# A two-layer hybrid diffusion backbone on one core: the first norm's modulation made wholly on TensorE, and the later modulation rows placed behind the input norms

## The chip, the cores and the metric

The kernel runs on one core of a Trainium2 chip as one launch. The metric is the device time of the launch in microseconds (us). Engines are named as in the profile: PE (TensorE), DVE (VectorE), ACT (ScalarE), POOL (GpSimd), and SP (SyncE), whose queue issues nearly all DMA transfers.

## What is computed

Two trunk layers run over 1024 latent tokens and 256 context tokens of width 1024, all in float32. Each layer begins with an RMS norm whose result is scaled and shifted by vectors that come from a conditioning vector (`c` for the latent tokens, `c_ctx` for the context tokens) through the matrix `w_mod`; then a combined input projection feeds four head groups (a short gated convolution, multi-head latent attention, a Conformer convolution, 2-D neighbourhood attention), an output projection merges them, and a squared-ReLU MLP follows.

```python
mod = [m[:, None, :] for m in jnp.split(jax.nn.silu(c) @ w_mod[i] + b_mod[i], N_MOD, axis=-1)]
mod_c = jnp.split(jax.nn.silu(c_ctx) @ w_mod[i] + b_mod[i], N_MOD, axis=-1)
x, xc = trunk_layer(x, xc, mod, mod_c, p, ang_row, ang_col, last=(i == DEPTH - 1))

# in trunk_layer
sh1, sc1, ga1, sh2, sc2, ga2 = mod
h = rmsnorm(x, p["g_pre_mix"]) * (1 + sc1) + sh1      # first norm
hc = rmsnorm(xc, p["g_pre_mix"]) * (1 + sc1c) + sh1c
u = h @ w_in
...
kv = heads(rmsnorm(ckv, g_kv) @ w_ukv)                 # latent keys: norm, then expansion
...
x = x + ga1 * rmsnorm(y, p["g_post_mix"])
hm = rmsnorm(x, p["g_pre_mlp"]) * (1 + sc2) + sh2
x = x + ga2 * rmsnorm(sq_relu_mlp(hm, p["w_mlp1"], p["w_mlp2"]), p["g_post_mlp"])
```

The product with `w_mod` gives 6 x 1024 numbers for each of two vectors and each layer: 48 tiles of 128. Tiles 0 to 15 are the shift and scale of the first norm; tiles 16 to 47 are wanted behind the attention. The change concerns layer 0.

## The kernel before

The tokens are kept transposed (channels on the 128 partitions, tokens along the free axis) in three segments of 512, 512 and 256 tokens (0, 1 and 2; the third is the context). Weights are split into a high and a low part, so that each product is three matmuls: `weights` loads 128x512 pieces into the ring of tiles `raw` (4 buffers), ScalarE writes the high part `wh`, GpSimd or VectorE the low part `wl`.

The modulation is made in two ways. `mod_pe` does tiles 0 to 6 on PE: for each tile a load of 512 KB into a tile `s` and eight matmuls of 128x2 (L246), and at the end one VectorE addition for each vector (L251). `mod_rows` does the others as row sums on VectorE (L288): for each tile two halves of 128x512 are loaded (L284), and for each half and each vector one scalar_tensor_tensor multiplies the half with a row of silu(c) that stands on all partitions (tiles `ya`) and adds up the row; tiles 7 to 15 use buffers of tag `s`, tiles 16 to 47 use tag `xl` (3 buffers). The rows in `ya` are made from a 4 KB load, four matmuls against ones (L264) and four Silu on ScalarE (L265).

A norm (`modulate`) squares x on ScalarE (L133), adds the squares up on VectorE (L148), sums over partitions on PE (L161), takes the root and reciprocal (L164, L165), broadcasts it on PE (L170), and then does for each of eight k-tiles two VectorE steps (L192, L194) with a ScalarE step between (L193); the trunk's matmuls read what these leave.

`layer` merges the stages: `merge` runs a main generator and lets others go on in proportion to its progress, by the numbers in RATES (`ma`, `mf`, `mv`, `mp`, `hm` belong to the modulation rows `moda`). The stage `first` holds the gate projections of segment 0 (L375 to L377) and the projection NQ of segment 0 (`na_project`, evacuated with L93 and L94 to `ge` and `pt`); behind it come the other segments, `values`, the latent projections with their norms (`mla_project`), and the heads. The instructions are emitted in this order, and a scheduler then sorts them by its own estimate of times before they are put into each engine's queue; each engine runs its queue in order. SP's queue too is in order: a load whose buffer isn't free holds up the loads behind it.

Of the kernel before, what the change touches and what calls it, by code (L numbers as in the profile page):

```python
# [6 lines left out]
AF = mybir.ActivationFunctionType  # L7
ALU = mybir.AluOpType
# [19 lines left out]
QTAG = 'xl'  # L28
PA, PD = 0, 1
WALT = (3, 2)  # L30
MPE, RM, MX = 7, 1.0, 4
ROT0, ROT1, ROT2 = 'SGSGS', 'SGSGS', 'SGSGS'
RATES = dict(pend=(1.0, 1.0), cv=(1.0, 0.862), cp=(1.0, 0.6), hr=(1.0, 0.484), hc=(0.3, 0.3), hm=(0.313, 0.679), ma=(0.195, 0.26), mf=(0.5, 0.5), mv=(0.5, 1.04), cb=(1.0, 1.3), mp=(0.5, 0.5), ar=(0.392, 0.517), ac=(0.6, 0.8), ob=(0.65, 0.696), oc=(0.575, 0.65), od=(0.65, 0.26), on=(0.6, 0.522), mb=(1.0, 0.646), pr=(0.2, 0.2), pt=(0.805, 1.12), pn=(0.612, 1.5), pm=(1.5, 1.5), mn=(1.74, 2.0), mc=(0.4, 0.325), mt=(1.0, 0.6), en=(1.0, 1.0))
PADC = 15
CFW = PADC + LAT + PADC + CTX + PADC
T5 = 1328
# [25 lines left out]
class Kern:  # L62
# [137 lines left out]
    def norm(self, y, si, o, n, l, which, acc, xsrc, xdst, nxt=None, ptag="R", tag="e2", tmp=None):  # L200
# [31 lines left out]
        if nxt:  # L232
            l2, w2, H = nxt
            yield n / 200
            yield from self.modulate(yk, n, l2, w2, v, H, o, acc, ptag, tag, tmp)


    def mod_pe(self, load):

        nc = self.nc  # L240
        ps = self.ps("O", [P, MPE, 2])
        for m in range(MPE):
            raw = self.t([P, KT, P], "s")
            nc.sync.dma_start(raw, self.a["wmod0"][m])
            for k in range(KT):
                nc.tensor.matmul(ps[:, m, :], raw[:, k, :], self.sc[:, k, :], start=k == 0, stop=k == KT - 1)  # L246
            if m == MX:
                load()
            yield 1.0
        for v in range(2):  # L250
            nc.vector.tensor_tensor(self.mods[0][v][:, 0:MPE], ps[:, :, v], self.vec[:, 0, 0:MPE], op=ALU.add)  # L251

    def mod_vectors(self, tags, pe=False):

        nc = self.nc
        out = []
        for v in range(2):
            t = self.t([P, 2, 512], tags[v])
            if pe:
                row = self.t([1, 1024], "s")  # L260
                nc.sync.dma_start(row, self.a["crow"][v:v + 1, :])
                for h in range(2):
                    ps = self.ps("S")
                    nc.tensor.matmul(ps, self.ones[0:1, :], row[:, h * 512:(h + 1) * 512], start=True, stop=True)  # L264
                    nc.scalar.activation(t[:, h], ps, AF.Silu)  # L265
                out.append([t[:, 0], t[:, 1]])
                continue
            nc.sync.dma_start(t, self.a["crow"][v:v + 1, :].rearrange("v (h c) -> v h c", h=2)
                              .to_broadcast([P, 2, 512]))
            nc.scalar.activation(t, t, AF.Silu)  # L270
            out.append([t[:, 0], t[:, 1]])
        return out

    def mod_rows(self, l, f0, f1, vecs, wtag="xl", jtag="ma"):

        nc = self.nc
        mod, part = self.mods[l], self.part
        nv = len(vecs)
        junk = self.t([P, 512], jtag) if nv > 1 else None
        a = f0  # L280
        for f in range(f0, f1):
            for h in range(2):
                w = self.t([P, 512], wtag)
                nc.sync.dma_start(w, self.a["wmodt"][l, f, :, h * 512:(h + 1) * 512])  # L284
                for v in range(nv):
                    dst = (mod if h == 0 else part)[v][:, f:f + 1]
                    q = w if v == nv - 1 else junk
                    nc.vector.scalar_tensor_tensor(q, w, 1.0, vecs[v][h], op0=ALU.mult, op1=ALU.mult,  # L288
                                                   accum_out=dst)
                yield nv * 0.6  # L290
            if f % 8 == 7 or f + 1 == f1:
                r = slice(a, f + 1)
                for v in range(nv):
                    nc.vector.tensor_tensor(mod[v][:, r], mod[v][:, r], part[v][:, r], op=ALU.add)
                    nc.vector.tensor_tensor(mod[v][:, r], mod[v][:, r], self.vec[:, l, r], op=ALU.add)
                a = f + 1
# [676 lines left out]
    def layer(self, l, H, pend):  # L973

        last = l == 1
        R = {k: v[l] for k, v in RATES.items()}
        qsegs = (0, 1) if last else (0, 1, 2)
# [4 lines left out]
        ch = self.chain  # L982
        self.cf_open(0)
        self.cf_open(1)
        moda = self.mod_rows(0, 16, 48, self.vecs) if l == 0 else iter(())
        first = ch(*[self.cf_gemm(l, H, (0,), j, j == 0 and l == 0) for j in range(2)], self.na_project(l, H, "NQ", M_NAQ, (0,)))
        if l:
            first = ch(first, self.na_project(l, H, "NK", M_NAK, (0,)))
        self.merge(first, (pend, R['pend']), (moda, R['ma']))
        self.go(pend)  # L990
        self.merge(self.cf_gemm(l, H, bsegs, 0), (moda, R['mf']))
        conv = ch(*[self.cf_conv(l, qsegs, j) for j in range(2)])
        self.merge(self.cf_gemm(l, H, bsegs, 1), (conv, R['cb']), (moda, R['mf']))
        self.merge(self.values(l, H), (conv, R['cv']), (moda, R['mv']))
        self.mla_open()
        self.merge(self.mla_project(l, H, (0, 1, 2), qsegs), (conv, R['cp']), (moda, R['mp']))
        heads = self.mla_heads(l, qsegs)
        rest1 = ch(self.na_project(l, H, "NK", M_NAK, (1, 2) if l else (0, 1, 2)), self.na_project(l, H, "NQ", M_NAQ, bsegs))
        self.merge(heads, (rest1, R['hr']), (conv, R['hc']), (moda, R['hm']))
        self.go(moda)  # L1000
        self.rot = "G"
        self.yfalloc(0)
# [103 lines left out]
    @staticmethod  # L1106
    def stats(g):

        next(g)
        next(g)  # L1110
# [7 lines left out]
    def run(self):  # L1118
# [39 lines left out]
        def load(si, tag):  # L1158
            o, n = SEGS[si]
            X[si] = Seg(pools[tag], n, F32, tag, f"x{si}")  # L1160
            for i, t in enumerate(X[si].tiles):
                kk = X[si].kk
                nc.sync.dma_start(t, a["xin"][:, i * kk:(i + 1) * kk, o:o + n])

        self.vecs = self.mod_vectors(("ya", "ya"), True)
        md = self.mod_rows(0, MPE, 16, self.vecs, wtag="s")
        H, first = {}, []

        def early():
            load(0, "ah")  # L1170
            g = self.modulate(X[0].k, 512, 0, "1", 0, lambda: H[0], 0, tmp="T")
            self.stats(g)
            first.append(g)
            self.w0 = [self.weights(a["win"][0, m], D) for m in (M_CFG, M_CFA)]

        self.merge(self.mod_pe(early), (md, RM))
        self.go(md)
        load(1, "c5")
        load(2, "ah")
        H.update({si: self.newh(SEGS[si][1]) for si in range(3)})  # L1180
        self.go(first[0])
        pend = self.chain(*[self.modulate(X[si].k, SEGS[si][1], 0, "1", int(si == 2), H[si], 0, ptag="O", tmp="T") for si in (1, 2)])
        H, pend = self.layer(0, H, pend)
        self.layer(1, H, pend)
# [103 lines left out]
```

## Time and profile before

| what | value |
|---|---|
| runs | 3201.49, 3206.51, 3210.8 us; median 3206.51 |
| the profiled execution | 3201.57 us, span 3199.6 us |
| PE busy | 2959.4 us (92%) |
| DVE busy | 2019.0 us (63%) |
| ACT busy | 1399.5 us (44%) |
| POOL busy | 1076.6 us (34%) |
| mean granted TensorE clock | 0.961 of full speed |

The span is from the first to the last instruction of the profiled execution. The busy shares are averages over stages of different make.

### The profile page before, as it was taken

The numbers are of one execution on the slowest core, as the hardware profiler recorded it, in microseconds if no ns is written. First come the engines' busy times: TensorE is split into PE (matmuls) and PEld (weight loads), VectorE is DVE, ScalarE is ACT, GpSimd is POOL, SyncE is SP. The second block draws the span as 40 slices with busy tenths as digits, with TensorE's granted clock in tenths as the row PEclk, the third lists the DMA queues.
The fourth block names the chain that finished last, engine by engine and source line by source line (L and its number), as shares of the span: only waits on it lengthen the run. The fifth ranks groups of instructions, "written<-read, shape, count | busy, mean of one in ns | idle before, by whom it ended". The sixth has DMA issues, their size and how long they took to land.

```text
span 3199.6 us, 46244 instructions
## 1 busy us (share of the span) xinstructions
PE 2959.4 (92%) x15916; PEld 2534.7 (79%) x15916; DVE 2019.0 (63%) x4128; ACT 1399.5 (44%) x2882; POOL 1076.6 (34%) x861
## 2 busy tenths in 40 slices
PE   7879889979999989889999998998989999989997
PEld 5767668878888878768888887777878888978886
DVE  8999556685753377975543689556776633654335
ACT  3313445666553364212322443555765433543332
POOL 2302122225444432223333421222334444334443
PEclk9889889989999989999999999998989999999998
DMA  7435423453533354563212443425445333534233
GB/s 264 152 120 189 118 62 101 126 148 107 159 109 96 102 186 150 193 213 107 91 60 66 145 140 126 141 76 144 151 116 146 111 96 96 172 100 147 96 97 104
DMA packets 284461, 410.01 MB, mean 128 GB/s; under 512 B 28098, under 2 KB 129474, under 8 KB 284228
## 3 DMA queue, kind: packets, MB, share of 16 engines
q1 hardware_dynamic: 284228, 407.07, 40.9%
q8 instruction: 126, 2.06, 0.3%
q14 instruction: 107, 0.88, 0.1%
HBM read 354.66 MB, written 52.30 MB: 127 GB/s over the span
## 4 chain that ended last, share of the span: by engine, by line
PE 70%; DVE 9%; DMA 5%; ACT 2%; issue 2%; SPq 1%; POOL 0%; DVEq 0%; ACTq 0%; POOLq 0%
PE G L122 11%; PE G L123 11%; PE G L124 11%; PE S L122 9%; PE S L124 9%; PE S L123 9%; PE T L675 3%; DMA xl<-in_wmodt_dram 2%; PE O L688 1%; PE O L687 1%; DVE xl L288 1%; DMA ah<-KR 1%; PE S L809 1%; PE S L758 1%; PE S L759 1%
## 5 line engine op out<-in xcount | busy, mean ns | idle before, releaser
L94 POOL TENSOR_TENSOR wl<-raw,wh 128x512 fp32r<-128x512 f32 x672 | 898.4, 1340 | 1525.7 <-ACT wh L93 1399.1
L93 ACT ACTIVATE wh<-raw 128x512 fp32r<-128x512 f32 x768 | 483.0, 631 | 847.7 <-PE S L123 391.9
L122 PE MATMUL G<-h,wh 128*128 128x512 f32 (+1 forms) x1128 | 427.0, 379 | 6.5 <-ACT h L193 2.3
L123 PE MATMUL G<-h,wh 128*128 128x512 f32 (+1 forms) x1128 | 423.0, 375 | 4.4 <-DVE h L194 4.3
L124 PE MATMUL G<-h,wl 128*128 128x512 f32 (+1 forms) x1128 | 423.4, 375 | 0.2 <-POOL wl L94 0.2
L122 PE MATMUL S<-h,wh 128*128 128x512 f32 (+1 forms) x904 | 324.6, 359 | 2.9 <-ACT h L193 1.6
L124 PE MATMUL S<-h,wl 128*128 128x512 f32 (+1 forms) x904 | 324.7, 360 | 1.4 <-POOL wl L94 1.4
L123 PE MATMUL S<-h,wh 128*128 128x512 f32 (+1 forms) x904 | 323.7, 358 | 0.0
L659 POOL TENSOR_SCALAR ah<-ah,sm 128x1280 f32<-128x1280 f32 (+3 forms) x144 | 148.2, 1033 | 410.4 <-DVE sm L658 155.2
L929 DVE TENSOR_TENSOR ac<-ac,S 128x512 f32<-128x512 f32 (+1 forms) x340 | 208.9, 617 | 114.6 <-PE S L124 113.7
L122 PEld LDWEIGHTS G<-h,wh 128*128 128x128 f32 x1128 | 215.7, 191 | 46.0 <-ACT h L193 4.7
L123 PEld LDWEIGHTS G<-h,wh 128*128 128x128 f32 x1128 | 215.2, 191 | 42.2 <-DVE h L194 6.0
L124 PEld LDWEIGHTS G<-h,wl 128*128 128x128 f32 x1128 | 215.4, 191 | 36.4 <-issue 0.7
L94 DVE TENSOR_TENSOR pt<-T,pt 128x512 fp32r<-128x512 f32 (+1 forms) x280 | 169.3, 615 | 87.9 <-ACT pt L93 86.6
L929 DVE TENSOR_TENSOR ac<-ac,G 128x512 f32<-128x512 f32 (+1 forms) x268 | 169.0, 631 | 82.1 <-PE G L124 80.9
L93 ACT ACTIVATE pt<-T 128x512 fp32r<-128x512 f32 (+1 forms) x280 | 146.5, 543 | 117.5 <-PE T L675 103.4
L122 PEld LDWEIGHTS S<-h,wh 128*128 128x128 f32 x904 | 173.9, 192 | 29.5 <-ACT h L193 2.3
L124 PEld LDWEIGHTS S<-h,wl 128*128 128x128 f32 x904 | 173.6, 192 | 27.3 <-POOL wl L94 2.7
L123 PEld LDWEIGHTS S<-h,wh 128*128 128x128 f32 x904 | 173.9, 192 | 25.6
L122 PE MATMUL G<-s,wh 128*128 128x512 f32 (+1 forms) x534 | 185.3, 348 | 2.2 <-ACT ge L863 1.7
L124 PE MATMUL G<-s,wl 128*128 128x512 f32 (+1 forms) x534 | 182.0, 341 | 3.3 <-DVE wl L94 3.2
L123 PE MATMUL G<-s,wh 128*128 128x512 f32 (+1 forms) x534 | 182.0, 341 | 0.3 <-DVE s L94 0.3
(339 smaller groups left out, 6938.9 us busy)
## 6 DMA issues: line engine op xcount, KB each, us to landing
raw<-in_w_dram SPq DMA_DIRECT2D x520, 256.0 KB, 2.6
xl<-in_wmodt_dram SPq DMA_DIRECT2D x160, 256.0 KB, 3.0
raw<-in_wout_dram SPq DMA_DIRECT2D x144, 256.0 KB, 3.0
raw<-in_win_dram SPq DMA_DIRECT2D x96, 256.0 KB, 3.1
ah<-KN SPq DMA_DIRECT2D x32, 320.0 KB, 4.9
ah<-MV SPq DMA_DIRECT2D x16, 640.0 KB, 6.4
ah<-NV SPq DMA_DIRECT2D x16, 640.0 KB, 4.9
XM<-yo SPq DMA_DIRECT2D x36, 256.0 KB, 2.9
```

Source lines behind the costliest of these rows:

```text
L93: nc.scalar.activation(hi, src, AF.Copy)
L94: (eng or nc.vector).tensor_tensor(lo, src, f32(hi), op=ALU.subtract)
L122: nc.tensor.matmul(out, wh, xh, start=i == 0, stop=False)
L123: nc.tensor.matmul(out, wh, xl, start=False, stop=False)
L124: nc.tensor.matmul(out, wl, xh, start=False, stop=i == last)
L288: nc.vector.scalar_tensor_tensor(q, w, 1.0, vecs[v][h], op0=ALU.mult, op1=ALU.mult, accum_out=dst)
L659: nc.gpsimd.tensor_scalar(p[:, :L], p[:, :L], sm[:, 9:10], 1.0, op0=ALU.mult, op1=ALU.mult)
L675: nc.tensor.transpose(T[:, i, q * P:(q + 1) * P], ps_list[q][:, cols[q]:cols[q] + P], self.ident)
L687: nc.tensor.matmul(O[:, a:b], V[:, kt, :], th[:, i, a:b], start=first, stop=False)
L688: nc.tensor.matmul(O[:, a:b], V[:, kt, :], tl[:, i, a:b], start=False, stop=last)
L758: nc.tensor.matmul(S, Qt[:, 0, q:q + P], K[0][:, ks], start=True, stop=False)
L929: nc.vector.tensor_tensor(a, a, ps, op=ALU.add)
```

## The change

`mod_pe` does all 16 tiles of the first norm (MPE = 16), 72 matmuls more; the 36 row sums of tiles 7 to 15 go. x0 is loaded at step 2 of `mod_pe` and its statistics are begun at step 12. The rows of silu(c) are made from a broadcast load of 512 KB each and one Silu of 128x1024 each, emitted behind the first norm. The modulation rows of tiles 16 to 47 take their buffers from the ring `raw`, aren't merged into the stage `first` or its pending norms any more, run at rates of their own (MODA; in RATES their entries were ma 0.195, mf 0.5, mf 0.5, mv 0.5, mp 0.5 and hm 0.313 for layer 0), and are kept in the order of the program on VectorE (`pin`).

```diff
-MPE, RM, MX = 7, 1.0, 4
+MPE, MX, MS = 16, 2, 12
+MODA = (1.0, 0.5, 0.5, 0.5, 0.3)
...
+    def pin(self, ins):
+
+        return self.tc.keep_in_program_order(ins)
+
-    def mod_pe(self, load):
+    def mod_pe(self, steps):
...
-            if m == MX:
-                load()
-            yield 1.0
+            if m in steps:
+                steps[m]()
...
-    def mod_vectors(self, tags, pe=False):
+    def mod_vectors(self, tags):
...
-            if pe:
-                row = self.t([1, 1024], "s")
-                nc.sync.dma_start(row, self.a["crow"][v:v + 1, :])
-                for h in range(2):
-                    ps = self.ps("S")
-                    nc.tensor.matmul(ps, self.ones[0:1, :], row[:, h * 512:(h + 1) * 512], start=True, stop=True)
-                    nc.scalar.activation(t[:, h], ps, AF.Silu)
-                out.append([t[:, 0], t[:, 1]])
-                continue
             nc.sync.dma_start(t, self.a["crow"][v:v + 1, :].rearrange("v (h c) -> v h c", h=2)
                               .to_broadcast([P, 2, 512]))
             nc.scalar.activation(t, t, AF.Silu)
...
-                    nc.vector.scalar_tensor_tensor(q, w, 1.0, vecs[v][h], op0=ALU.mult, op1=ALU.mult,
-                                                   accum_out=dst)
+                    self.pin(nc.vector.scalar_tensor_tensor(q, w, 1.0, vecs[v][h], op0=ALU.mult, op1=ALU.mult,
+                                                            accum_out=dst))
...
-        moda = self.mod_rows(0, 16, 48, self.vecs) if l == 0 else iter(())
+        moda = self.mod_rows(0, 16, 48, self.vecs, "raw") if l == 0 else iter(())
...
-        self.merge(first, (pend, R['pend']), (moda, R['ma']))
+        self.merge(first, (pend, R['pend']))
         self.go(pend)
-        self.merge(self.cf_gemm(l, H, bsegs, 0), (moda, R['mf']))
+        self.merge(self.cf_gemm(l, H, bsegs, 0), (moda, MODA[0]))
...
-        self.merge(heads, (rest1, R['hr']), (conv, R['hc']), (moda, R['hm']))
+        self.merge(heads, (rest1, R['hr']), (conv, R['hc']), (moda, MODA[4]))
...
-        self.vecs = self.mod_vectors(("ya", "ya"), True)
-        md = self.mod_rows(0, MPE, 16, self.vecs, wtag="s")
         H, first = {}, []
 
-        def early():
-            load(0, "ah")
+        def stats():
             g = self.modulate(X[0].k, 512, 0, "1", 0, lambda: H[0], 0, tmp="T")
             self.stats(g)
...
-        self.merge(self.mod_pe(early), (md, RM))
-        self.go(md)
+        self.mod_pe({MX: lambda: load(0, "ah"), MS: stats})
...
         self.go(first[0])
+        self.vecs = self.mod_vectors(("ya", "ya"))
```

Three places of the queues, as the scheduler leaves them. The lines of the changed kernel are its own numbers (L149 is L148 of before, L193 is L192, L283 is L288, L103 is L102).

**VectorE at the start, changed kernel.** `e_495` is the sum of x1's squares, `mod_127` and `mod_128` the vectors of the latent and the context tokens, `g` their gains, `T` the first norm's first step:

```order
L149 TENSOR_TENSOR e_495<-e_495,e_506 128x512
L149 TENSOR_TENSOR e_495<-e_495,e_509 128x512
L149 TENSOR_TENSOR e_495<-e_495,e_512 128x512
L149 TENSOR_TENSOR e_495<-e_495,e_515 128x512
L255 TENSOR_TENSOR mod_127<-O_133,vec 128x16
L255 TENSOR_TENSOR mod_128<-O_133,vec 128x16
L308 SCALAR_TENSOR_TENSOR g_395<-mod_127,vec 128x8
L308 SCALAR_TENSOR_TENSOR g_755<-mod_128,vec 128x8
L193 SCALAR_TENSOR_TENSOR T_397<-x_0_164,g_395,e_303 128x512
L193 SCALAR_TENSOR_TENSOR T_401<-x_0_164,g_395,e_303 128x512
```

In the kernel before, the additions of the vectors stood ahead of most of these sums, with row sums between them; now the two additions (L255) and the first norm stand behind x1's whole sum.

**ScalarE at the same place, changed kernel.** `e_` are x1's squares, `ya_429` and `ya_432` the rows of silu(c), `h_0` the first norm's result:

```order
L134 ACTIVATE e_509<-x_2_365 128x512
L134 ACTIVATE e_512<-x_3_366 128x512
L265 ACT_TABLE_LOAD
L265 ACTIVATE ya_429<-ya_429 128x1024
L134 ACTIVATE e_515<-x_3_366 128x512
L265 ACTIVATE ya_432<-ya_432 128x1024
L174 ACTIVATE e_303<-G_295 128x512
L194 ACTIVATE h_0_375<-T_397,mod_127 128x512
```

The last square of x1 stands between the two Silu.

**VectorE at the third segment's input norm, before.** `h_0_402` and `T_781` belong to this norm, `ma` and `xl` to modulation rows:

```order
L194 SCALAR_TENSOR_TENSOR h_3_399<-T_696,mod_127,h_3_395 128x512
L165 RECIPROCAL sm_773<-sm_773 128x2
L288 SCALAR_TENSOR_TENSOR xl_1164,mod_128<-xl_1164,ya_142 128x512
L288 SCALAR_TENSOR_TENSOR ma_532,part_131<-xl_1221,ya_133 128x512
L167 TENSOR_TENSOR e_776<-ident,sm_773 128x256
L288 SCALAR_TENSOR_TENSOR xl_1221,part_132<-xl_1221,ya_142 128x512
L288 SCALAR_TENSOR_TENSOR ma_532,mod_127<-xl_1225,ya_133 128x512
L288 SCALAR_TENSOR_TENSOR xl_1225,mod_128<-xl_1225,ya_142 128x512
L192 SCALAR_TENSOR_TENSOR T_781<-x_0_380,g_779,O_770 128x256
L192 SCALAR_TENSOR_TENSOR T_785<-x_0_380,g_779,O_770 128x256
```

**and in the changed kernel**, where `c_439` is an evacuation of the gates, `pt_667` and `pt_741` are the two evacuations of NQ, and the norm is that of `h_0_393`:

```order
L360 TENSOR_TENSOR c_439<-S_587,c_439 128x4x16x8
L195 SCALAR_TENSOR_TENSOR h_3_390<-T_676,mod_127,h_3_386 128x512
L95 TENSOR_TENSOR pt_667<-G_641,ge_666 128x512
L95 TENSOR_TENSOR pt_741<-S_715,ge_740 128x512
L166 RECIPROCAL sm_749<-sm_749 128x2
L168 TENSOR_TENSOR e_752<-ident,sm_749 128x256
L193 SCALAR_TENSOR_TENSOR T_757<-x_0_371,g_755,O_746 128x256
L193 SCALAR_TENSOR_TENSOR T_761<-x_0_371,g_755,O_746 128x256
L195 SCALAR_TENSOR_TENSOR h_0_393<-T_757,mod_128,h_0_391 128x256
L195 SCALAR_TENSOR_TENSOR h_0_393<-T_761,mod_128,h_0_391 128x256
L193 SCALAR_TENSOR_TENSOR T_765<-x_0_371,g_755,O_746 128x256
```

The row sums between the steps are gone, and the norm follows the second evacuation of NQ directly. The rows begin 16 instructions further on, behind the norm's last step.

**SP's queue at the key/value expansion's weights, before:**

```order
L284 DMA xl_1721<-in_wmodt_dram 128x512
L102 DMA raw_1995<-in_win_dram 128x512
L284 DMA xl_1725<-in_wmodt_dram 128x512
L102 DMA raw_2128<-in_wukv_dram 128x512
L284 DMA xl_1729<-in_wmodt_dram 128x512
L102 DMA raw_2144<-in_win_dram 128x512
```

**and in the changed kernel**, where `in_wmodt` are the modulation rows' loads:

```order
L279 DMA raw_2040<-in_wmodt_dram 128x512
L279 DMA raw_2044<-in_wmodt_dram 128x512
L279 DMA raw_2083<-in_wmodt_dram 128x512
L279 DMA raw_2087<-in_wmodt_dram 128x512
L279 DMA raw_2121<-in_wmodt_dram 128x512
L279 DMA raw_2125<-in_wmodt_dram 128x512
L103 DMA raw_2129<-in_wukv_dram 128x512
L103 DMA raw_2145<-in_win_dram 128x512
```

Of four buffers in the ring `raw`, the tile `raw_2129` takes the one that `raw_2083` leaves.

## Rows read from the trace of the kernel before

**Rows 1.** The busy time of each engine in four stretches and over all of them (view by stretches): the stretch, its length, the busy time and instruction count of each engine, the granted TensorE clock, the share of the DMA engines, GB/s.

```profile
0.00:54.40 54.40, 36.14 (x135) 29.52 (x136) 41.10 (x112) 17.67 (x29) 7.37 (x10) 1.00 0.90 325
54.40:134.20 79.80, 65.60 (x255) 48.52 (x256) 79.77 (x181) 33.68 (x58) 26.86 (x16) 0.89 0.47 150
134.20:240.00 105.80, 88.19 (x496) 77.99 (x495) 105.80 (x252) 21.07 (x51) 12.10 (x8) 0.90 0.39 125
240.00:357.20 117.20, 98.88 (x486) 82.00 (x485) 94.40 (x191) 36.73 (x78) 21.23 (x16) 0.90 0.54 178
0.00:357.20 357.20, 288.81 (x1368) 238.03 (x1369) 321.07 (x732) 109.14 (x216) 67.56 (x50) 0.91 0.53 178
```

**Rows 2.** The same view for the modulation rows alone (line 288 on VectorE; the accumulator read that belongs to each has its own record): the stretch, its length, VectorE busy with them and their records.

```profile
0.00:54.40 54.40, 30.13 (x81) 1.00 0.90 325
54.40:134.20 79.80, 43.63 (x103) 0.89 0.47 150
134.20:240.00 105.80, 42.25 (x116) 0.90 0.39 125
240.00:357.20 117.20, 12.19 (x30) 0.90 0.54 178
```

**Rows 3.** The timeline, around 22 to 30 us: start, duration, engine, line, operation, tiles, count. One row of GpSimd's casts and two modulation rows of VectorE.

```profile
22.41 6.49 POOL L94 TENSOR_TENSOR wl<-raw,wh 128x512 fp32r<-128x512 f32 x4 [21.47 <-ACT wh L93]
...
24.34 1.75 DVE L288 SCALAR_TENSOR_TENSOR ma<-s,ya 128x512 f32<-128x512 f32 x1
...
29.48 0.69 DVE L288 SCALAR_TENSOR_TENSOR s<-s,ya 128x512 f32<-128x512 f32 x1
```

**Rows 4.** The timeline: the matmuls of the first norm's vectors, the sums and broadcast of its statistics, and the first norm's start.

```profile
15.17 13.81 PE L246 MATMUL O<-sc,s 128*128 128x2 f32 x64
...
37.38 2.05 PE L170 MATMUL G<-e,ones 128*128 128x512 f32 x2
...
53.41 1.83 PE L161 MATMUL O<-ones,e 128*128 128x1 f32 x8 [13.98 <-DVE e L148]
...
54.49 1.41 DVE L192 SCALAR_TENSOR_TENSOR T<-x,g,e 128x512 f32<-128x512 f32 x2
...
55.44 1.26 ACT L193 ACTIVATE h<-T,mod 128x512 fp32r<-128x512 f32 x2
...
56.17 0.80 PE L375 MATMUL S<-h,wh 128*128 128x512 f32 x1 [0.93 <-ACT h L193]
...
56.58 1.17 ACT L93 ACTIVATE ah<-ah 128x1152 fp32r<-128x1152 f32 x1
```

**Rows 5.** The DMA view of 0 to 60 us: GB/s in 40 equal slices of 1.5 us, and two of the loads (KB of one, median us to landing).

```profile
GB/s 0 121 125 330 303 382 408 352 415 404 400 389 384 403 411 423 410 391 392 373 388 385 378 393 386 388 362 352 381 411 415 397 158 12 0 141 128 81 171 4
...
x<-in_xin_dram SPq DMA_DIRECT2D x10, 512.0 KB, 8.9
...
s<-in_wmod_dram SPq DMA_DIRECT2D x7, 512.0 KB, 6.8
```

**Rows 6.** The timeline: squares on ScalarE and their additions on VectorE, x0.

```profile
16.84 1.15 ACT L133 ACTIVATE e<-x 128x512 f32<-128x512 f32 x2 [0.96 <-DMA x<-in_xin_dram]
...
18.02 3.12 DVE L148 TENSOR_TENSOR e<-e,e 128x512 f32<-128x512 f32 x4 [0.54 <-ACT e L133]
```

**Rows 7.** The timeline of TensorE: successive matmuls of the trunk at three places (the spacing is the difference of the starts).

```profile
59.34 0.63 PE L377 MATMUL G<-h,wl 128*128 128x512 f32 x1
59.76 0.63 PE L375 MATMUL S<-h,wh 128*128 128x512 f32 x1
...
89.28 0.39 PE L122 MATMUL G<-h,wh 128*128 128x512 f32 x1
89.51 0.39 PE L123 MATMUL G<-h,wh 128*128 128x512 f32 x1
...
146.44 0.28 PE L122 MATMUL S<-h,wh 128*128 128x256 f32 x1
146.56 0.28 PE L123 MATMUL S<-h,wh 128*128 128x256 f32 x1
```

**Rows 8.** The timeline of VectorE: steps of the third segment's input norm (256 columns), one early and the last.

```profile
118.20 0.87 DVE L192 SCALAR_TENSOR_TENSOR T<-x,g,O 128x256 f32<-128x256 f32 x2
...
133.34 0.86 DVE L194 SCALAR_TENSOR_TENSOR h<-T,mod,h 128x256 fp32r<-128x256 f32 x2
```

**Rows 9.** The timeline: the load of the key/value expansion's weights, the third latent-norm step, and the first softmax of attention with the matmul before it.

```profile
150.00 0.33 SPq L102 DMA_DIRECT2D raw<-in_wukv_dram  x1
...
239.52 0.41 DVE L167 TENSOR_TENSOR e<-ident,sm 128x256 f32<-128x256 f32 x1
...
356.27 0.40 PE L758 MATMUL S<-ah,xl 96*128 96x512 f32 x1
...
357.18 0.69 DVE L645 TENSOR_REDUCE sm<-S 128x1 f32<-128x512 f32 x1 [0.46 <-PE S L760]
```

**Rows 10.** What VectorE waited for in 240 to 357 us: line waited by, what it waited for, us in total, times, longest.

```profile
DVE pt L94 <- ACT ge L93: 13.4, 5, 6.8
DVE ma L288 <- DMA xl<-in_wmodt_dram: 5.3, 4, 2.4
```

**Rows 11.** The view by stretches for the convolution's steps alone (line 402 on VectorE).

```profile
134.20:240.00 105.80, 54.55 (x89) 0.90 0.39 125
```

More of the change, by code (lines that the diff above doesn't have):

```diff
@@ L30 @@
 WALT = (3, 2)
-MPE, RM, MX = 7, 1.0, 4
+MPE, MX, MS = 16, 2, 12
+MODA = (1.0, 0.5, 0.5, 0.5, 0.3)
 ROT0, ROT1, ROT2 = 'SGSGS', 'SGSGS', 'SGSGS'
-RATES = dict(pend=(1.0, 1.0), cv=(1.0, 0.862), cp=(1.0, 0.6), hr=(1.0, 0.484), hc=(0.3, 0.3), hm=(0.313, 0.679), ma=(0.195, 0.26), mf=(0.5, 0.5), mv=(0.5, 1.04), cb=(1.0, 1.3), mp=(0.5, 0.5), ar=(0.392, 0.517), ac=(0.6, 0.8), ob=(0.65, 0.696), oc=(0.575, 0.65), od=(0.65, 0.26), on=(0.6, 0.522), mb=(1.0, 0.646), pr=(0.2, 0.2), pt=(0.805, 1.12), pn=(0.612, 1.5), pm=(1.5, 1.5), mn=(1.74, 2.0), mc=(0.4, 0.325), mt=(1.0, 0.6), en=(1.0, 1.0))
+RATES = dict(pend=(1.0, 1.0), cv=(1.0, 0.862), cp=(1.0, 0.6), hr=(1.0, 0.484), hc=(0.3, 0.3), cb=(1.0, 1.3), ar=(0.392, 0.517), ac=(0.6, 0.8), ob=(0.65, 0.696), oc=(0.575, 0.65), od=(0.65, 0.26), on=(0.6, 0.522), mb=(1.0, 0.646), pr=(0.2, 0.2), pt=(0.805, 1.12), pn=(0.612, 1.5), pm=(1.5, 1.5), mn=(1.74, 2.0), mc=(0.4, 0.325), mt=(1.0, 0.6), en=(1.0, 1.0))
 PADC = 15
@@ L988, in layer @@
             first = ch(first, self.na_project(l, H, "NK", M_NAK, (0,)))
-        self.merge(first, (pend, R['pend']), (moda, R['ma']))
+        self.merge(first, (pend, R['pend']))
         self.go(pend)
-        self.merge(self.cf_gemm(l, H, bsegs, 0), (moda, R['mf']))
+        self.merge(self.cf_gemm(l, H, bsegs, 0), (moda, MODA[0]))
         conv = ch(*[self.cf_conv(l, qsegs, j) for j in range(2)])
-        self.merge(self.cf_gemm(l, H, bsegs, 1), (conv, R['cb']), (moda, R['mf']))
-        self.merge(self.values(l, H), (conv, R['cv']), (moda, R['mv']))
+        self.merge(self.cf_gemm(l, H, bsegs, 1), (conv, R['cb']), (moda, MODA[1]))
+        self.merge(self.values(l, H), (conv, R['cv']), (moda, MODA[2]))
         self.mla_open()
-        self.merge(self.mla_project(l, H, (0, 1, 2), qsegs), (conv, R['cp']), (moda, R['mp']))
+        self.merge(self.mla_project(l, H, (0, 1, 2), qsegs), (conv, R['cp']), (moda, MODA[3]))
         heads = self.mla_heads(l, qsegs)
         rest1 = ch(self.na_project(l, H, "NK", M_NAK, (1, 2) if l else (0, 1, 2)), self.na_project(l, H, "NQ", M_NAQ, bsegs))
-        self.merge(heads, (rest1, R['hr']), (conv, R['hc']), (moda, R['hm']))
+        self.merge(heads, (rest1, R['hr']), (conv, R['hc']), (moda, MODA[4]))
         self.go(moda)
```

## The prediction

> **What bounds the kernel now.** The page comes first: TensorE is busy 2959.4 of 3199.6 us, so over the whole program it is the bound. But the change touches only layer 0 up to its first attention, and an average over the program says nothing of that stretch. So the second view is the table by stretches, cut at the first norm's start (54.4), the end of the third input norm (134.2), the third latent-norm step (240) and the first softmax (357.2) [rows 1]. There VectorE is the bound: 41.10 of 54.40, then 79.77 of 79.80 and 105.80 of 105.80, then 94.40 of 117.20. Between 54.4 and 240 us it has no idle time at all; before that it has 13.3 us, after it 22.8. TensorE has 50 us of gaps between 54.4 and 357.2 (302.8 less 65.6, 88.2 and 98.9). The same table for the modulation rows alone [rows 2] shows what fills VectorE: 128.20 us in 330 records, two for each of 164 instructions (one cut by a boundary counts in both stretches), 0.78 us each on average; 0.73 in the third stretch (42.25 for 58), 0.85 in the second (43.63 for 51.5). So up to the first softmax the time is VectorE's work plus VectorE's waits, and I sum the change that way; behind the softmax nothing is changed, and I let the difference pass through as it stands.
>
> **The change, part by part.**
>
> *36 row sums leave VectorE.* Tiles 7 to 15 had 9 x 2 x 2 of them. At 0.73 that is 26.3 us, at 0.85 it is 30.6. I take 0.73. The longer ones are the ones that met a GpSimd instruction: 1.75 us beside GpSimd's cast of the weights, 0.69 just behind it [rows 3]. GpSimd casts the same weights after the change, so what is taken away is the plain part. The Trainium skill ("SBUF — State Buffer", section "SBUF: two separate sides") says that a VectorE instruction with two SBUF inputs and a GpSimd instruction that reads SBUF exclude each other for a whole instruction, whichever began second waiting; the 1.75 agrees. By that rule the stretching goes over to the next such VectorE instruction and is not saved, which speaks against counting the 0.85.
>
> *72 matmuls of 128x2 come to TensorE.* One costs 13.81/64 = 0.216 us [rows 4], so all 16 tiles cost 27.6 us. In the new order TensorE does 4 tiles, waits for the sum of x0's squares, does 8 column sums (1.83), 9 tiles, two broadcasts (2.05) and 3 tiles. x0's sum: 3 tiles of wmod and 4 of x are 3.7 MB; the DMA moved 1.3 MB by 7.5 us and then about 0.59 MB per 1.5 us [rows 5], so x0 is there at some 14 us and summed at 16. From there 1.8 + 15.6 + 2.1 + 5.2 gives 41 us. This is hidden if the vectors are not wanted before 41; without that cover each tile would cost 1.7 us.
>
> *When the first norm can start.* In VectorE's new order the 7 additions of x1's squares stand ahead of the two additions that finish the vectors. Bytes ahead of x1's last tile: 16 wmod (8.4 MB), x0 (2.1), four weights (1.05), x1 (2.1), 13.6 MB in all: 7.5 + 12.3/0.394 = 39 us. A second thing is later. On ScalarE the last of x1's eight squares stands behind the Silu of the broadcast c row, and that row lies behind two context tiles and itself in the queue, 15.2 MB: 43 us. Then a Silu of 1024 columns (a 1152-wide ScalarE copy takes 1.17 [rows 4]), a square and an addition (0.58 and 0.78 at the pace of [rows 6]): some 46. The vectors and gains follow, so the first norm begins at 47 us, and the first trunk matmul, 1.7 us behind it as before (54.49 to 56.17 [rows 4]), at 49 to 50 against 56.17. Six to seven us are won on TensorE. VectorE has 14 additions and little else by then, 11 us of work, so it has idled 36.
>
> *The input norms without rows between them.* Before, two row sums stood between most norm steps, and VectorE was never out of work. Now none stands ahead of the last norm step of segment 2, and the third segment's norm stands behind the evacuation of the second NQ block in VectorE's order. That evacuation needs 144 of the trunk's 512-wide matmuls, and the third norm's broadcast another 24 behind them: 169 x 0.23 = 38.9 us at the pace of [rows 7], so 49.5 + 38.9 = 88, and 1 to 2 more for TensorE's waits for the first eight norm steps. Then 16 steps at 0.43 (two in 0.87 [rows 8]) with their handovers, 7 to 9 us: the norms end at about 99, against 134.2 before. VectorE's work in 47 to 99 is 32 wide steps of 0.7 (two in 1.41 [rows 4]), 16 narrow ones and about 12 small ones, 36 us; with the 11 before it has 47, and has idled 52 of 99. At this point it had idled 13.3 before. So 38.7 us more idle.
>
> *The rows behind it.* The 128 rows of tiles 16 to 47 all still come before the first softmax, as before: their work moves and is neither more nor less. They now take their buffers from the ring of four that the weights use. This is a new wait. The weights of the key/value expansion were loaded at 150.0 us, long before use [rows 9]; in the new order of SyncE's queue they stand behind tile 2083 in the ring, whose rows are about 40 instructions behind the third latent-norm step on VectorE. No row of before shows this wait. From below: VectorE sees nothing of it, since it is behind and TensorE catches up, 0. From above: 42 rows of 0.65 (27 us), DMA and casts of 5, less some 15 of matmuls that TensorE has between the two places: 17 per such place, and TensorE's stall counts only as far as VectorE then waits for it. I take 5. SyncE is in order, so what stands behind the waiting load (the writes of KN, further weights) waits with it; it is in the same price.
>
> *Sum.* Idle +38.7, work -26.3, ring +5: +17.4 us. The idle time of 240 to 357, 22.8 us, most of it for casts behind TensorE (13.4 [rows 10]), I leave as it is. A second way: norms end at 99; then up to the third latent-norm step VectorE has 82 rows of 0.73, 160 convolution steps of 0.613 (54.55/89 [rows 11]) and some 10 us more, so it is there at 267 (before: 239.5 [rows 9], with 149 rows and 93 convolution steps done). From there the old VectorE had 94.4 us of work [rows 1]; the new one has 46 rows left where the old had 15 (+23) and 26 convolution steps where the old had 93 (-41), so 76. TensorE has 271 matmuls of 512 columns and 188 of 256 from there to the first attention: at 0.23 and 0.12 [rows 7] 85 us. So TensorE is the longer there, and with 15 to 25 of waits (the old kernel took 117 for 79 us of such matmuls, but there VectorE had 94 us to do beside them) the softmax comes at 367 to 377, +10 to +20. I stay with the sum.
>
> The profiled execution took 3201.57 us (span 3199.6), 4.9 below the median of the runs, 3206.5. I add to the median: 3206.5 + 17.4 = 3224.
>
> **The rivals.** A measurement of this kernel tells about 0.3% (9.6 us) from no change.
>
> *Faster.* The earlier first matmul carries through, and the third norm is not held by NQ: if the norms end at 80, VectorE has idled 33 and the sum is 33 - 13.3 - 26.3 = -7; with the clock 10 less, 3190 to 3200. It decides at an end of the norms of 86.6, where the new idle equals 13.3 + 26.3. For it: the first 20 trunk matmuls ran at 0.43 us each, which is 1.2 GHz, against 0.23 later [rows 7], with a granted share of 0.89 in that stretch [rows 1]; with TensorE busy up to its start this could be 3 us less. Against it: VectorE's order is fixed. The Trainium skill ("TensorE: Matmul & The Clock Gate", section "Why this matters for your kernels") advises no idle gaps between bursts of matmuls; by that rule the added matmuls help, but TensorE waits here too between 41 and 49.
>
> *No change.* The stall at the seam is half what I think (norms end at 90), and no load waits in the ring: 43 - 39.6 = +3, 3210. For it: TensorE's gaps (50 us) can take up what comes late.
>
> *Slower still.* The shared ring stops TensorE and VectorE in turn, at the weights of the latent keys, the two query blocks and the expansion, 17 us each, partly overlapping: +30, 3237. For it: several weights in SyncE's order stand behind pinned rows. Against it: where VectorE is far behind, the wait is its own work.
>
> **How the numbers follow.** Forecast 0.42, slower still 0.18, no change 0.27, faster 0.13. The forecast's own range is 3214 to 3232. The range reaches to the faster case's near edge and beyond the slower still: 3197 to 3243. Faster by over 0.3%: most of the faster case, 0.12. Slower: the forecast, the slower still and a part of no change would be 0.6; same 0.28.
>
> **What the profile after would show.** First trunk matmul at 49 to 50 us; the two vector additions behind x1's last square; VectorE idle some 17 us between 47 and 99, waiting for TensorE's NQ block; no row before the third norm's last step; the third latent-norm step at about 267; weight loads whose issue waits for VectorE; the first softmax at 367 to 377. I would be wrong if VectorE has other work to fill the seam, if the norms end before 87, or if the idle time of 240 to 357 shrinks by as much as the early idle grows.

## The result, and the profile after

The changed kernel takes 3241.74 us (median of four runs, 3238.63 to 3244.5) against 3204.7 for the kernel before beside it: a ratio of 1.0113, with an interval of 1.0094 to 1.0132, 37 us slower. Its profiled execution took 3238.63 us, span 3236.8. The number lies inside the predicted range and the sign is the forecast one, but the step is twice the forecast 17.4, and the ledger below shows that it came about in another way: 54 us are lost by the first softmax, 29 come back in the MLP, and some 14 go again in layer 1.

The view by stretches answers to [rows 1]; the cuts are the first norm's start, the end of the third input norm, the third latent-norm step and the first softmax.

```profile
0.00:65.36 65.36, 58.23 (x267) 57.17 (x267) 11.16 (x25) 19.11 (x28) 5.66 (x10) 1.00 0.75 283
65.36:117.38 52.02, 50.26 (x204) 40.36 (x205) 39.07 (x71) 32.42 (x55) 19.13 (x12) 0.96 0.25 83
117.38:282.98 165.60, 98.62 (x524) 84.76 (x524) 156.43 (x366) 23.03 (x54) 12.94 (x10) 0.75 0.31 100
282.98:411.56 128.58, 104.34 (x513) 86.48 (x512) 81.01 (x194) 38.09 (x79) 23.67 (x18) 0.89 0.61 197
```

VectorE's work up to the softmax is 287.7 us, 33.4 less than the 321.1 of before. Its idle time is 54.2, 13.0, 9.2 and 47.6 us, 124 in all, against 36. So 87.8 more idle less 33.4 work is the 54.4 us by which the softmax is later. TensorE was starved in the third stretch, 98.6 busy of 165.6 at a granted clock of 0.75; in the first two it idles 7.1 and 1.8 us, and in the last 24.2. The modulation rows alone, in the last two stretches of after, to be read beside [rows 2] (in the first two they have 0.07 us):

```profile
117.38:282.98 165.60, 56.34 (x164) 0.75 0.31 100
282.98:411.56 128.58, 33.14 (x92) 0.89 0.61 197
```

The timeline of the start answers to [rows 4]:

```profile
6.69 13.78 PE L251 MATMUL O<-sc,s 128*128 128x2 f32 x64 [6.69 <-DMA s<-in_wmod_dram]
...
22.04 30.86 PE L251 MATMUL O<-sc,s 128*128 128x2 f32 x144
...
47.87 0.69 DVE L149 TENSOR_TENSOR e<-e,e 128x512 f32<-128x512 f32 x1 [2.19 <-ACT e L134]
...
54.60 10.24 PE L251 MATMUL O<-sc,s 128*128 128x2 f32 x48
...
64.88 0.26 DVE L255 TENSOR_TENSOR mod<-O,vec 128x16 f32<-128x16 f32 x2 [16.32 <-PE O L251]
65.36 1.42 DVE L193 SCALAR_TENSOR_TENSOR T<-x,g,e 128x512 f32<-128x512 f32 x2
...
66.98 0.77 PE L370 MATMUL S<-h,wh 128*128 128x512 f32 x1
```

x1's last addition is at 47.87, close to the 46 of the forecast. But the two additions of the vectors wait 16.3 us more for TensorE: it has 64 + 144 + 48 = 256 records, of 0.215 us each, for the program's 128 matmuls. The third group of rows answers to [rows 9]:

```profile
282.98 0.41 DVE L168 TENSOR_TENSOR e<-ident,sm 128x256 f32<-128x256 f32 x1
...
307.93 0.33 SPq L103 DMA_DIRECT2D raw<-in_wukv_dram  x1
...
411.56 0.69 DVE L640 TENSOR_REDUCE sm<-S 128x1 f32<-128x512 f32 x1 [0.43 <-PE S L755]
```

The expansion's weights are loaded at 307.9 instead of 150.0. The waits of 117 to 283 us (line waiting, what it waited for, us in total, times, longest) show the ring that the prediction spoke of: TensorE waits for the high part of a weight, and SP's queue for VectorE to leave a tile. TensorE's first, then SP's two longest:

```profile
PE S L123 <- ACT wh L94: 48.8, 3, 29.9
```

```profile
SPq L279 <- DVE raw L283: 88.4, 26, 13.4
SPq L103 <- DVE raw L283: 21.7, 9, 3.7
```

And VectorE's main wait in 283 to 411.5 us, to be read beside [rows 10]:

```profile
DVE pt L95 <- ACT ge L94: 38.2, 13, 7.3
```

Behind the softmax, the two kernels are followed by landmarks that both traces have on VectorE. The changed kernel is later by 54.4 us at the softmax, 51.3 at the last broadcast of the output norms of layer 0, 22.6 at layer 1's first norm, 24.4 at layer 1's first softmax, and 37.1 at its last instruction. So between the second and third of these, in the MLP, it gains 29 us. The stretch as a whole, of before and of after:

```profile
1187.60:1570.50 382.90, 353.86 (x1985) 307.05 (x1986) 270.75 (x591) 119.43 (x243) 109.83 (x81) 0.96 0.46 149
```

```profile
1238.90:1593.10 354.20, 345.48 (x1985) 302.07 (x1986) 266.72 (x593) 119.87 (x243) 115.24 (x81) 0.98 0.50 161
```

The same number of matmuls, in 29 us less: TensorE idles 9 us there instead of 29, and its busy time is 8 us shorter at a granted clock of 0.98 instead of 0.96.

### The profile page after: what moved, and what is told of

Same layout as the page of the kernel before. It is cut to its first block, busy times and chain, and to the rows that moved or that the text cites. A ratio compares the mean times of both kernels' runs of the same rounds, so it can differ in the third digit from the quotient of the medians.

```text
span 3236.8 us, 46444 instructions
## 1 busy us (share of the span) xinstructions
PE 2981.7 (92%) x16052; PEld 2566.8 (79%) x16052; DVE 1974.8 (61%) x4048; ACT 1403.2 (43%) x2882; POOL 1074.2 (33%) x861
## 4 chain that ended last, share of the span: by engine, by line
PE 70%; DVE 8%; DMA 4%; ACT 2%; issue 2%; SPq 1%; POOL 0%; ACTq 0%; DVEq 0%; POOLq 0%
PE G L123 11%; PE G L124 11%; PE G L125 11%; PE S L123 9%; PE S L125 9%; PE S L124 9%; PE T L670 3%; DMA ah<-KR 2%; PE O L683 1%; PE O L682 1%; PE S L804 1%; PE S L754 1%; PE S L755 1%; PE S L753 1%; DVE xl L283 1%
## 5 line engine op out<-in xcount | busy, mean ns | idle before, releaser
L123 PE MATMUL S<-h,wh 128*128 128x512 f32 (+1 forms) x904 | 327.1, 362 | 50.9 <-ACT wh L94 48.8
```

What stands on the lines that cost most here:

```text
L123: nc.tensor.matmul(out, wh, xh, start=i == 0, stop=False)
```

## The experiments

Times stand beside runs of the kernel before on the same chip (3199 to 3200 us there); at the ratio of 1.0113 the changed kernel would take 3235 to 3236 on these. "Softmax" is the first one of layer 0.

**e1, layer 1's rows unpinned.** The pin sits in a helper that layer 1's modulation rows use as well, in the MLP of layer 0.

```diff
-                    self.pin(nc.vector.scalar_tensor_tensor(q, w, 1.0, vecs[v][h], op0=ALU.mult, op1=ALU.mult,
-                                                            accum_out=dst))
+                    ins = nc.vector.scalar_tensor_tensor(q, w, 1.0, vecs[v][h], op0=ALU.mult, op1=ALU.mult,
+                                                         accum_out=dst)
+                    if l == 0:
+                        self.pin(ins)
```

> The changed kernel, with the pin kept for layer 0's modulation rows and dropped for layer 1's, which the same helper issues. In the trace after, the first softmax is 54 us later than before but the MLP of layer 0's first segment (1299 to 1593) takes 294 us against 323, and the end is 37 us later. Theory P (the pin on layer 1's rows, which spreads them over the MLP, gives these 29 us back): the MLP stretch takes 323 us again and the time is 3242 + 25 to 32, about 3270. Rival (the stretch is shorter for another reason, such as where the loads fall after a later start): the time stays within 6 us of 3242.

Measured: 3256.85 us, ratio 1.0177 (1.0158 to 1.0196), some 21 us above the changed kernel. The MLP stretch is back at 380.7 us, 26.5 longer than in the changed kernel:

```profile
1240.10:1620.80 380.70, 354.87 (x1985) 308.53 (x1986) 270.59 (x591) 119.52 (x243) 111.59 (x81) 0.96 0.45 149
```

Theory P holds for the stretch. The time rose by less than the 25 to 32 us expected, since layer 1 takes 8 us less here (1632 against 1640 from its first norm to the end).

**e2, the kernel before with layer 1's rows pinned.** The same lines, in the kernel before, with `if l == 1`.

> The kernel before, with the pin on layer 1's modulation rows alone and nothing else changed. Theory P: the MLP stretch falls from 323 to about 294 us; up to 8 of it is lost again in layer 1's attention as it was in the changed kernel, so 3205 - 20 to 29, about 3180. Rival (another reason for the shorter stretch): 3205, no change beyond 0.3%.

Measured: 3187.25 us, ratio 0.9959 (0.9945 to 0.9972). The MLP stretch takes 355.5 against 382.9:

```profile
1186.50:1542.00 355.50, 345.96 (x1985) 302.12 (x1986) 265.29 (x592) 120.23 (x243) 114.95 (x81) 0.98 0.49 160
```

So the pin on layer 1's rows is worth 27 us there by itself. Without it the 128 rows run from 1275.7 to 1446.3 us, with it from 1301.5 to 1521.9: they are spread more thinly. TensorE's largest wait for VectorE in the old stretch is gone with the pin; before it was:

```profile
PE G L122 <- DVE c L94: 15.5, 4, 5.7
```

That the thinner spread ends this wait fits both traces; no run varies the spread by itself. In the end 14 of the 27 are lost in layer 1 (more on this below), so the time falls by 12 us, where 20 to 29 were expected.

**e3, the later rows back in tag xl.**

```diff
-        moda = self.mod_rows(0, 16, 48, self.vecs, "raw") if l == 0 else iter(())
+        moda = self.mod_rows(0, 16, 48, self.vecs) if l == 0 else iter(())
```

> The changed kernel, with layer 0's later modulation rows in buffers of tag xl as before instead of the weights' ring. Theory R (the shared ring makes TensorE wait for weights, 60 us in the trace after, and VectorE wait behind it in turn): TensorE's wait for wh between 113 and 412 falls from 60 to under 10 us, VectorE's idle there falls by 25 to 40, the first softmax comes at 370 to 390 instead of 411.6, and the time is 3242 - 20 to 40, about 3210. Rival (VectorE is the bound in that stretch, and TensorE's wait is only VectorE's backlog under another name): the first softmax stays within 8 us of 411.6 and the time within 8 of 3242.

Measured: 3220.8 us, ratio 1.0065 (1.0051 to 1.0078), 15 less than the changed kernel; softmax at 400.2, third latent norm at 280.8. Theory R was half right. TensorE's waits for weights are gone, but the gain is below the 20 to 40 us expected, and the stretch from 117 to 281 us is only 2 us shorter than in the changed kernel:

```profile
117.18:280.79 163.61, 93.61 (x538) 83.51 (x537) 163.29 (x375) 23.56 (x54) 14.62 (x10) 0.77 0.30 102
280.79:400.17 119.38, 100.43 (x488) 82.83 (x488) 77.98 (x184) 36.92 (x77) 21.82 (x16) 0.89 0.63 208
```

```profile
PE G L619 <- DVE e L614: 60.3, 1, 60.3
```

VectorE is now busy 163.3 of 163.6, and TensorE waits 60.3 us in one piece for the rotated keys (L614) in place of 48.8 for weights. The wait for weights there was VectorE's backlog under another name. The ring was a cost of its own mainly behind the latent norm, where 9 of the 11 us at the softmax are won.

**e4, half of the vectors' matmuls.** It leaves out half of the contraction, and is for the time alone.

```diff
-            for k in range(KT):
+            for k in range(KT // 2):
```

> The changed kernel, with half of the contraction of the first norm's vectors left out (4 matmuls for each tile instead of 8). The trace after has 256 matmul records for 128 of the program, 3.43 us for each tile, 55 us in all, where the prediction counted 27.6. Theory M (TensorE's vectors set the first norm's start): the first trunk matmul comes at 49 to 51 us instead of 67.0, held by the addition of x1's squares, and the time falls by 12 to 17 us to about 3228. Rival (the ring and VectorE's fixed order behind it take up an earlier start): the start is as early, but the time stays within 5 us of 3242.

Measured: 3217.21 us, ratio 1.0052 (1.0038 to 1.0067), 18 less. The first trunk matmul comes even sooner than expected, since the order changed and most of x1's additions now stand behind the vectors:

```profile
44.65 0.80 PE L370 MATMUL S<-h,wh 128*128 128x512 f32 x1 [2.54 <-ACT h L194]
```

The softmax is at 395.1, 16.5 earlier. Theory M holds, with 18 us where 12 to 17 were expected; part of it may come from the changed order and not from the matmuls.

**e5, both of these.** It leaves out the same half.

> The changed kernel with both edits: half of the contraction of the first norm's vectors left out, and layer 0's later rows in buffers of tag xl. Alone, the first brought the first softmax from 411.6 to 395.1 and the second to 400.2. Theory (two separate causes that add up): the first softmax at 381 to 387, the time 18 + 14 below the changed kernel, about 3203 beside a kernel before of 3199, and about 27 us of the delay at the softmax left for the placement of the rows. Rival (one cause hides behind the other): the softmax stays at 392 to 398.

Measured: 3194.53 us, ratio 0.9985 (0.9975 to 0.9995), softmax at 376.7. The two causes don't hide each other, but they aren't separate either: together they give 35 us at the softmax, where 16.5 and 11.4 were had singly; a softmax at 381 to 387 was expected. Without the ring, half of the vectors' matmuls is worth 23.5 (e5 beside e3). The softmax is still 20 us later than before, though TensorE starts 12 us earlier.

**e6, only the placement and the pin, in the kernel before.** Tiles 0 to 6 on TensorE, tag xl.

```diff
-        self.merge(first, (pend, R['pend']), (moda, R['ma']))
+        self.merge(first, (pend, R['pend']))
...
-        self.merge(self.cf_gemm(l, H, bsegs, 0), (moda, R['mf']))
+        self.merge(self.cf_gemm(l, H, bsegs, 0), (moda, MODA[0]))
...
+                    if l == 0:
+                        self.pin(ins)
```

> The kernel before (7 tiles on TensorE, rows of tiles 7 to 15 on VectorE from the start, tag xl), with only the placement of the change: layer 0's rows of tiles 16 to 47 not merged into the first stage, the new rates, and the pin on layer 0's rows; layer 1's are not pinned. Theory S (the placement leaves VectorE without work beside the norms and with too little between the third latent norm and the softmax): the norms end near 105 instead of 134, VectorE idles 10 to 17 us there and 15 to 25 more than 22.8 before the softmax, the first softmax comes at 382 to 398 and the time is 3199 + 25 to 40. Rival (only the late first norm of the changed kernel costs; the placement is free): the first softmax within 6 us of 357 and the time within 8 of 3199.

Measured: 3235.16 us, ratio 1.011 (1.0093 to 1.0127); softmax at 389.0, 31.8 later.

```profile
0.00:59.84 59.84, 38.82 (x140) 31.03 (x140) 35.75 (x107) 18.57 (x32) 6.79 (x10) 1.00 0.80 291
59.84:112.70 52.86, 49.22 (x205) 39.24 (x206) 38.67 (x70) 31.82 (x54) 21.05 (x14) 1.00 0.27 92
112.70:277.45 164.75, 94.08 (x543) 84.01 (x542) 164.44 (x381) 23.56 (x54) 14.71 (x10) 0.77 0.29 101
277.45:388.96 111.51, 95.30 (x483) 79.38 (x482) 74.47 (x180) 36.22 (x77) 22.30 (x16) 0.91 0.67 222
```

VectorE idles 24.1, 14.2, 0.3 and 37.0 us. Theory S holds, though the norms end at 112.7 and not near 105, and the last stretch idles 14 us more than before instead of 15 to 25: the placement with its pin does most of the damage. This run doesn't tell the two apart; e9 and e10 do.

**e7, only 16 tiles on TensorE, in the kernel before.**

```diff
-MPE, RM, MX = 7, 1.0, 4
+MPE, RM, MX = 16, 1.0, 4
```

> The kernel before with one number changed: 16 tiles of the first norm's modulation on TensorE instead of 7; rows of tiles 16 to 47 stay where the old kernel has them. TensorE's 256 matmul records take 55 us, so the first norm starts at about 65 instead of 54.5. Theory V (VectorE's work and idle time make the time up to the first softmax): VectorE has 26 to 30 us less to do and idles 20 to 28 us more before the first norm, as it can draw only some of the later rows ahead; the softmax comes at 350 to 362 and the time is 3199 - 5 to + 5. Rival T (TensorE's later start is what counts): the softmax at 366 to 370 and the time 3199 + 9 to 13.

Measured: 3222.08 us, ratio 1.0072 (1.0055 to 1.0089). The first norm starts at 71.8, not 65, and the softmax is at 364.8, 7.6 later, between the two theories. The time is above both: 14 of the 23 us come in layer 1 (below). VectorE's rows up to the softmax, 36 fewer in their old placement:

```profile
0.00:364.78 364.78, 98.42 (x256) 0.92 0.50 175
```

**e8, the same with layer 1's rows pinned.**

> The kernel of the run before with the pin on layer 1's rows added, which gave 28.6 us in the MLP of layer 0 and 12 us at the end. If the two are independent, the time is that of the run before less 12 to 28 us: 3172 to 3190, and it may be below the kernel before with the pin alone (3187). If VectorE's order in layer 1 depends on the start, the gain of the pin is gone and the time equals that of the run before.

Measured: 3190.27 us, ratio 0.9969 (0.9958 to 0.998), 32 less than e7 where 12 to 28 were expected. The pin's gain is there, and a little more; it isn't better than e2.

**e9, the changed kernel with layer 0's rows unpinned.** As e1, with `if l == 1`.

> The changed kernel with the pin kept for layer 1's modulation rows and dropped for layer 0's. In VectorE's order 160 convolution steps and 82 rows stood ahead of the third latent norm with the pin (before the change 93 and 149); without it 95 and 95 do. Theory Q (the pin in layer 0 lets the convolution, which nobody wants yet, go ahead of the latent norm that TensorE waits for, and leaves too little behind it): the third latent norm comes some 30 us earlier, at 245 to 262 instead of 283, the first softmax at 375 to 400 instead of 411.6, and the time is 10 to 35 below the changed kernel's 3235 on such a chip. Rival (the rows' late emission alone does it, pinned or not): the softmax within 6 us of 411.6 and the time within 8 of 3235.

Measured: 3198.1 us, ratio 0.9988 (0.9977 to 0.9999); softmax at 368.5 instead of 411.6, third latent norm at 242.2 instead of 283.0.

```profile
0.00:65.33 65.33, 58.23 (x267) 57.17 (x267) 11.15 (x25) 19.13 (x28) 5.66 (x10) 1.00 0.75 283
65.33:132.78 67.45, 59.93 (x258) 48.04 (x259) 62.80 (x134) 34.88 (x59) 25.55 (x16) 0.92 0.38 131
132.78:242.19 109.41, 89.96 (x500) 78.41 (x499) 109.05 (x264) 20.98 (x51) 11.44 (x8) 0.88 0.38 131
242.19:368.50 126.31, 101.67 (x485) 84.48 (x484) 107.68 (x233) 36.94 (x78) 19.77 (x16) 0.86 0.56 184
```

Theory Q holds, with more than was expected: 43 us at the softmax instead of 12 to 37, and some 37 in the time instead of 10 to 35. Up to the latent norm VectorE has 24 us less to do (183.0 instead of 206.7), since 65 of the convolution's steps come behind it instead of ahead of it, and idles 17 us less (59.2 instead of 76.3), since 31 rows again run beside the input norms. Behind it VectorE has 107.7 us to do instead of 81.0 and idles 18.6 instead of 47.6, so that the convolution's steps fill time that stood empty.

**e10, and the later rows in tag xl as well.**

> The run before with layer 0's later rows in buffers of tag xl as well. VectorE's order then has 57 rows ahead of the third input norm and 122 rows and 101 convolution steps ahead of the third latent norm, close to the kernel with 16 tiles on TensorE and the old placement (softmax at 365, 3190 with layer 1 pinned). Theory Q with the ring's part: softmax at 360 to 375, time 3185 to 3200. Rival: the softmax stays near the run before's.

Measured: 3181.84 us, ratio 0.9948 (0.9931 to 0.9965), the fastest of all: softmax at 353.9, 3.3 earlier than before, and the MLP's gain. Both are better than expected (360 to 375, 3185 to 3200). Its interval overlaps that of e2, which has the pin on layer 1's rows and nothing else of the change; so it isn't shown that the rest of the change gives anything in the time.

```profile
0.00:67.67 67.67, 60.00 (x274) 58.85 (x274) 26.31 (x69) 20.65 (x30) 5.69 (x10) 1.00 0.84 312
67.67:143.85 76.18, 64.05 (x250) 47.12 (x251) 76.15 (x180) 33.70 (x57) 26.41 (x16) 0.91 0.46 154
143.85:247.80 103.95, 88.05 (x499) 78.04 (x498) 103.95 (x239) 21.54 (x52) 11.75 (x8) 0.90 0.34 117
247.80:353.87 106.07, 91.49 (x483) 76.41 (x482) 86.15 (x167) 36.42 (x77) 20.06 (x16) 0.95 0.55 187
```

VectorE has no idle time from the first norm to the third latent norm, as in the kernel before.

**e11 and e12, the two kernels once more.** The stretch from layer 1's first norm to the end differed between profiles by up to 15 us.

> The kernel before once more, unchanged, for a second profile. From layer 1's first norm to the end the profiles took 1625 (before), 1640 (changed), 1632, 1639, 1632, 1625, 1625, 1630, 1639 and 1634 us, with no order by pin, ring or tiles. If this spread belongs to the execution, the second profile may fall anywhere in 1625 to 1640 there, while the first softmax stays at 357 within 2 us. If it belongs to the kernel, it is 1625 again within 2.

> The changed kernel once more, unchanged, for a second profile. By the execution's spread: anywhere in 1625 to 1640 from layer 1's first norm to the end, the first softmax at 411.6 within 2. By the kernel: 1640 again within 2.

Measured: 1630 and 1643 us in that stretch (1625 and 1640 the first time), softmax at 357.0 and 412.1. With two profiles of each, an execution moves it by 3 to 5 us, and most of the 10 to 15 seems to belong to the kernel. It goes with neither pin, ring nor tiles (e4 and e5 have 1625, e7 without any pin 1639). What sets it stays open.

## Why the prediction was right or wrong, point by point

**What bounds the stretch: right for the middle of it only.** That VectorE's work and idle time add up to the softmax is true of any engine and shows nothing. VectorE is the bound where it has no idle time: from the first norm to the latent norm before and in e10, and in the third stretch of e3 and e6. In the changed kernel it idles 124 of 411.6 us, and TensorE is what it waits for at the start (16.3 us for the vectors) and, by way of ScalarE's copies, behind the latent norm (38.2).

**The first norm's start, 47 predicted, 65.4 measured: the cost of the matmuls was mis-sized.** The prediction divided 13.81 us by 64 and took 0.216 us for a matmul of the program. [Rows 4] have 64 records for 4 tiles, that is 16 for each tile of 8 matmuls; 7 tiles had 112 records in all. A tile costs 3.43 us, the 16 tiles 55 and not 27.6, and the cover that was named (x1's squares, up to 47) is too short. The count of records against the program's loop would have shown it. With half of these matmuls, which is what the prediction had priced, the softmax comes 16.5 us sooner (e4), or 23.5 without the ring (e5 beside e3); VectorE's order changed with it, so neither is the price of the matmuls alone.

**The row sums taken away, 26.3 predicted: right for the 36 rows, too little for the whole change.** The rows took 128.2 us before and take 89.5 now, 0.70 us each, so 38.7 less; VectorE's other work up to the softmax grew by 5.3, so 33.4 net. This made the forecast 7 us too slow. Where the same 36 rows go and the others keep their place (e7), rows fall by 29.8 and other work grows by 3.3, 26.5 net, as priced. The rest goes with the pin and the ring: the 128 rows take 89.5 us with both, 95.9 without the pin (e9), 94.2 without the ring (e3) and 98.5 without either (e10). The Trainium skill ("SBUF — State Buffer", section "SBUF: two separate sides") has the two engines exclude each other for a whole instruction. The 1.75 us of [rows 3] agree with it. Whether the growth of the other work is the stretching that passed over to it, as the prediction has it, is not shown by any run.

**The norms without rows between them: right.** 13.0 us of idle time were measured between the first norm and the third norm's end, where 17 were predicted; e6 has 14.2. VectorE waits there for the evacuations of NQ (6.0) and for the third norm's broadcast (3.6), as named. Idle up to the norms' end is 67.2, 15 more than the 52 predicted, from the late start.

**The rows behind it, "neither more nor less": the step that failed.** The prediction had counted 160 convolution steps ahead of the third latent norm, where before there were 93, and used them only in its second way. It left the idle time before the softmax at 22.8, as before; it is 47.6, and 41.4 without the ring (e3). The third stretch idles 9.2, of which 7.2 in one wait for TensorE. The pin is the cause of most of the step: with it VectorE does the convolution ahead of the latent norm that TensorE needs, TensorE starves, and behind the norm VectorE has too little beside it. Without the pin the softmax is 43 us earlier (e9 beside the changed kernel) or 46 (e10 beside e3). The second way, 367 to 377 for the softmax, had the right order of events but started 18 us early and took TensorE's matmuls behind the latent norm for 85 us. They keep it busy for 104.3 of 128.6, so that its waits of 24.2 are within the 15 to 25 given, and the price of the matmuls was 19 short.

**The ring, 5 us predicted: 11 at the softmax** (e3), 15 in the time. The rival "slower still" named TensorE and VectorE stopping in turn; the 48.8 us of waits were there, but e3 shows most of them to be VectorE's backlog, as the argument against that rival said. Its 3237 is the time nearest to the measured one, but only in part by its mechanism. Without the pin the ring costs 14.6 at the softmax (e9 less e10).

**"Behind the softmax nothing is changed": wrong.** The pin sits in a helper that layer 1 uses too, and gives back between 26 and 29 us in the MLP (e1, e2). Without it the time would be 1.0177 x 3204.7 = 3261, 37 above the forecast and outside the range. That the time fell into the range is luck: errors on the two sides of the softmax offset each other. Up to it the step is 37 us more than the 17.4 forecast: 15.2 of idle time up to the norms' end, 9.2 in the third stretch and 24.8 behind the latent norm, less 7.1 of work and the 5 taken for the ring. Behind it 29 come back and some 14 go again.

The step at the softmax, put together from the runs: the placement and the pin 31.8 (e6), all tiles on TensorE with the new start that goes with them 11.2 (e3 less e6), the ring 11.4: 54.4. In another order: all of the change without layer 0's pin and the ring -3.3 (e10), that pin 46.3 (e3 less e10), the ring 11.4. So without that pin and the ring the rest of the change, the placement in it, costs nothing at the softmax. Behind the softmax: the pin in layer 1, some -28, and 10 to 15 in layer 1 that stay open. The version that keeps what helps, layer 1's pin, without layer 0's and without the ring, is e10, 0.5% faster than the kernel before; layer 1's pin by itself gives 0.4% (e2).

## What to carry to other kernels

Before a record's duration is used as a price, the records are counted against the loop that issues them. A helper's other callers belong to the change: one line moved 27 us in a stage that the change didn't name. An order fixed by hand on one engine also fixes what gets ahead of it: the work to look at isn't only the pinned one, but what the scheduler puts in its place in front of an instruction that another engine waits for.

## What the runs showed of the hardware that was not expected

A float32 matmul of the program shows as two records, at 128x2 (256 records for 128 matmuls, 0.215 us each) and at 128x512 (the statistic's broadcast, two records in 2.05 us, beside 0.23 for one of the trunk's fp32r matmuls of the same size). And in the stretch in which TensorE was starved the granted clock fell to 0.75 of full speed (98.6 us busy of 165.6), against 0.90 where it was busy 88 of 106 [rows 1]. The 0.75 is a mean of two levels: 1.00 (2.4 GHz) from 157 to 197 us, where TensorE was busy throughout, and 0.50 (1.2 GHz) from 205 to 229, where it waited for a weight and did nothing. The first matmuls behind that wait, at 232 us, still follow each other at 0.43 us for 512 columns, and from 237 to 245 the clock is 1.00 again.

```profile
157.00:197.00 40.00, 40.00 (x289) 38.87 (x288) 39.24 (x97) 6.90 (x22) 2.58 (x2) 1.00 0.40 135
205.00:229.00 24.00, 0.00 (x0) 0.00 (x0) 23.48 (x52) 1.58 (x3) 0.00 (x0) 0.50 0.18 59
```

The Trainium skill ("TensorE: Matmul & The Clock Gate", section "Why this matters for your kernels") advises against idle gaps between bursts of matmuls; these stretches agree with it.
